# A gated MLP on one core: first casts, weight sums, operand steps and transposes moved to other places in program order

## The chip, the core and the metric

The kernel runs on one core of a Trainium2 chip. The metric is the device time of one execution in microseconds (us); medians and, where small differences matter, means of several executions are given, always beside executions of the kernel before in the same rounds. Every execution also lists the mean clock that was granted to the tensor engine (1.000 is full speed). Engines: PE is the tensor engine, DVE VectorE, ACT ScalarE, POOL GpSimd, SP SyncE, whose queue issues most DMAs.

## The reference

```python
def reference(x, w_gate, w_up, w_down):       # x: 8 x 1024 x 1024, weights 1024 x 4096 and 4096 x 1024
    gate = x @ w_gate
    up = x @ w_up
    gate = 0.5 * gate * (1 + np.tanh(np.sqrt(2 / np.pi) * (gate + 0.044715 * gate ** 3)))
    h = gate * up
    return (h @ w_down).astype(np.float32)
```

## The kernel before

Eight passes of 1024 tokens, each with a gate/up phase (16 pairs of column blocks, 14 products of four matmuls each) and a down phase. It uses fast matrix multiplication (fewer products, more sums): weights and x are added into "operands" first. The first three passes use seven-product sums and, on the side, make the operands for the later passes (w_ops, wd_quads in memory). All of it is scheduled by hand: instructions run on each engine in program order. The parts that the change touches:

The very first pair, before anything is prepared:

```python
def x0_transpose(mh, g, b):                   # PE transposes one block of x, two copies out of PSUM
    ...
    nc.vector.tensor_copy(xq["b11" if mh == 0 else "b12"][:, :, c], ps[:, 0:KH])
    nc.scalar.copy(xq["b21" if mh == 0 else "b22"][:, :, c], ps[:, KH : 2 * KH])

def cast_first(w, kh, cols):                  # float32 weights to float16, on ACT
    nc.scalar.copy(raw(0, 0)[:, w, kh * KH : (kh + 1) * KH, cols], staging0(w, kh)[:, :, cols])
...
for g in range(G):
    x0_transpose(0, g, 4 + g)
    warm(2 if g < G - 1 else 8)               # matmuls on ones, to keep PE's clock up
for kh in range(2):
    for w in range(2):
        cast_first(w, kh, slice(0, 256))
for kh in range(2):
    products(0, kh, slice(0, MH))             # the first 32 products, first half of K first
```

The sums of w_down in the first gate/up phase, placed by product number (14 per pair; `s0 = 28 * n + 59`):

```python
(21, wd_sums, (0,)), (22, wd_sums, (1,)),
(23, wd_sums, (2,)), (24, wd_sums, (3,)), (25, wd_store, (n,)),
```

The operand units of the second and third gate/up phase (a load, then 20 steps, one every six products):

```python
UNITS_ONE = {1: ((0, 60, 6),), 2: ((2, 20, 6),)}    # pass: (unit, product of the load, spacing)
    unit_steps[s0] = load
    unit_steps[s0 + 20 + ds * k] = f
```

The down phase (seven chains v of two chunks nb and four blocks g, one step of eight matmuls each):

```python
steps.setdefault(9 + (17 if i else 0) + 5 * k // 6, []).append(f)    # operand steps
...
if nb == 0 and g == 0 and p + 1 < NPASS:
    ...
    if v == (2 if p < FAST - 1 else 0):       # FAST is 3
        transpose_x(p + 1)                    # four DMA transposes of x on SP's queue
```

## Time and profile before

| | before |
|---|---|
| time, first three runs | 2269.1 us median, 2267.74 to 2269.33 |
| span of the profiled execution | 2265.6 us |
| PE busy | 2249.9 us |
| listed PE waits | 11.6 us, all before 740 us |
| the largest of them | 2.08 us at 389.8, second gate/up phase |

PE is busy nearly all the time, so the profile is read for PE's few waits and for the chain behind each. A wait list gives total, times and longest; the timeline shows in brackets how long an engine stood idle before an instruction and what ended it. The lines are in the prediction below.

### The profile page before, as it was taken

To read this page: it belongs to the slowest core of one execution; us is meant where nothing else is said; L and a number is where in the kernel's file an instruction comes from. 1 tells how busy PE (TensorE), PEld (TensorE's weight loads), DVE (VectorE), ACT (ScalarE), POOL (GpSimd) and SP (SyncE) were. 2 spreads that over 40 slices of the span, in tenths; PEclk is the share of its full clock that TensorE was granted. 3 is DMA by queue.
4 is the path that set the end of the run, shared out by engine and by line. 5 is a ranking of instruction groups with operands and counts; after the bars stand their busy time and mean duration, and the time that the engine had idled before them with its cause. 6 is when DMAs were issued, how large, how long until landed. Compare 5 with 4: busy or idle time off the path is not lost.

```text
span 2265.6 us, 42805 instructions
## 1 busy us (share of the span) xinstructions
PE 2249.9 (99%) x16639; PEld 1625.8 (72%) x16639; DVE 1560.5 (69%) x2188; ACT 956.5 (42%) x1868; POOL 687.4 (30%) x825
## 2 busy tenths in 40 slices
PE   9999999999999999999999999999999999999999
PEld 4444444444444445888888888888888888888888
DVE  5576457874488855777776668666776667866674
ACT  4443135551265522666125551255403553055520
POOL 1343013330133310454105450245402543034520
PEclk9999999999999999999999999999999999999999
DMA  9998969999999999999998989989999889998876
GB/s 232 177 209 205 250 209 223 247 264 284 254 242 238 263 313 342 332 343 373 306 334 279 316 310 303 334 272 322 296 328 321 280 314 312 324 314 277 283 290 228
DMA packets 308092, 642.45 MB, mean 284 GB/s; under 512 B 79088, under 2 KB 185328, under 8 KB 287344
## 3 DMA queue, kind: packets, MB, share of 16 engines
q1 hardware_dynamic: 253104, 566.57, 73.4%
q0 software_dynamic: 54784, 73.14, 19.2%
q8 instruction: 130, 2.13, 0.4%
q14 instruction: 74, 0.61, 0.1%
HBM read 574.36 MB, written 138.41 MB: 315 GB/s over the span
## 4 chain that ended last, share of the span: by engine, by line
PE 91%; DVE 5%; DMA 2%; SPq 1%; issue 1%; ACT 0%; POOL 0%; DVEq 0%; ACTq 0%
PE ps L847 40%; PE ps L1097 20%; PE ps L625 19%; PE ps L989 11%; DVE ring L350 2%; DVE tmp L644 1%; DMA x_sums<-in_w_down_dram 1%; SPq L255 1%; DVE h_s L278 1%; DMA wd_quads<-x_sums 1%; PE ps L1196 1%; DVE h_a L662 1%; DVE x_sums L278 0%; DMA h_a<-in_x_dram 0%; DMA ring<-wd_ops 0%
## 5 line engine op out<-in xcount | busy, mean ns | idle before, releaser
L847 PEld LDWEIGHTS <-ring 128*128 128x128 f16 x8320 | 814.1, 98 | 94.4
L824 POOL TENSOR_TENSOR h_a<-tmp 128x256 f16<-128x256 f32 x640 | 468.5, 751 | 840.1 <-ACT tmp L812 832.8
L847 PE MATMUL ps<-x_sums,ring 128*128 128x256 f16 x5760 | 655.8, 273 | 0.0
L809 DVE TENSOR_TENSOR tmp<-tmp,ps 128x512 f32<-128x512 f32 x640 | 414.4, 683 | 147.4 <-PE ps L847 101.6
L625 PEld LDWEIGHTS <-ring 128*128 128x128 f16 x2632 | 257.4, 98 | 319.4 <-issue 10.9
L794 ACT COPY tmp<-ps 128x512 f32<-128x512 f32 x520 | 303.9, 584 | 237.3 <-PE ps L847 159.5
L625 PE MATMUL ps<-x_sums,ring 128*128 128x512 f16 x1504 | 342.7, 379 | 5.9 <-DVE tmp L644 2.9
L812 ACT ACTIVATE tmp<-tmp 128x256 f32<-128x256 f32 x640 | 263.8, 418 | 173.3 <-DVE tmp L807 79.6
L847 PE MATMUL ps<-x_b,ring 128*128 128x256 f16 x2560 | 305.6, 273 | 0.0
L651 POOL TENSOR_TENSOR h_a<-tmp 128x512 f16<-128x512 f32 x94 | 153.4, 1632 | 375.1 <-ACT tmp L649 254.4
L807 DVE TENSOR_TENSOR tmp<-ps,tmp 128x512 f32<-128x512 f32 x240 | 165.4, 689 | 145.7 <-ACT tmp L794 100.0
L625 PE MATMUL ps<-x_b,ring 128*128 128x512 f16 x1128 | 259.1, 379 | 0.0
L1097 PEld LDWEIGHTS <-h_a 128*128 128x128 f16 x2240 | 219.2, 98 | 25.4
L989 PE MATMUL ps<-ring,h_a 128*128 128x512 f16 x1024 | 222.3, 379 | 0.4 <-DMA ring<-wd_ops 0.4
L1097 PE MATMUL ps<-ring,h_a 128*128 128x256 f16 x1920 | 216.1, 273 | 0.0
L644 DVE TENSOR_TENSOR tmp<-ps,tmp 128x512 f32<-128x512 f32 x188 | 127.4, 684 | 121.4 <-ACT tmp L636 118.5
L989 PEld LDWEIGHTS <-h_a 128*128 128x128 f16 x1152 | 112.7, 98 | 136.6 <-DMA ring<-wd_ops 0.9
L1154 ACT ACTIVATE tmp<-ps 128x512 f32<-128x512 f32 x60 | 35.3, 597 | 362.6 <-PE ps L1097 274.6
L1166 DVE SCALAR_TENSOR_TENSOR tmp<-ps,tmp 128x512 f32<-128x512 f32 x120 | 81.1, 690 | 97.5 <-PE ps L1097 66.7
L636 ACT COPY tmp<-ps 128x512 f32<-128x512 f32 x188 | 109.8, 585 | 86.4 <-PE ps L625 83.3
L350 DVE TENSOR_TENSOR ring<-ring 128x1024 f16<-128x1024 f16 x188 | 133.0, 721 | 9.3 <-DMA ring<-in_w_up_dram 5.1
L1097 PE MATMUL ps<-ring,x_sums 128*128 128x256 f16 x1120 | 126.4, 273 | 0.0
(100 smaller groups left out, 1536.6 us busy)
## 6 DMA issues: line engine op xcount, KB each, us to landing
ring<-w_ops SPq DMA_DIRECT2D x480, 512.0 KB, 5.0
ring<-wd_quads SPq DMA_DIRECT2D x110, 1024.0 KB, 7.0
ring<-wd_ops SPq DMA_DIRECT2D x35, 1024.0 KB, 7.4
out_dram<-tmp SPq DMA_DIRECT2D x128, 256.0 KB, 6.6
w_ops<-h_s SPq DMA_DIRECT2D x128, 256.0 KB, 7.0
ring<-in_w_gate_dram POOLq DMA_DIRECT2D x23, 1024.0 KB, 10.9
ring<-in_w_up_dram POOLq DMA_DIRECT2D x23, 1024.0 KB, 18.4
wd_quads<-x_sums SPq DMA_DIRECT2D x131, 128.0 KB, 5.7
```

What stands on the lines that cost most here:

```text
L350: nc.vector.tensor_tensor(o, a, b, op)
L625: nc.tensor.matmul(ps(b, w), lhs[:, k], rhs[:, k, :], start=(first and k == 0), stop=(k == KH - 1), skip_group_check=True,)
L644: nc.vector.tensor_tensor(o, ps("b", w), o, ADD)
L651: nc.gpsimd.tensor_tensor(hq[TO[n]][:, i, :], tmp[:, t[n, 1]], tmp[:, t[n, 0]], MUL)
L794: nc.scalar.copy(tmp[:, t[o[1]]], ps_all[:, bank[o[2]]])
L807: nc.vector.tensor_tensor(d, b, a, SUB)
L809: nc.vector.tensor_tensor(d, a, b, ADD if o[4] == "add" else SUB)
L812: nc.scalar.activation(d, d, GELU, scale=GSC)
L824: nc.gpsimd.tensor_tensor(h, tmp[:, t[o[1]], MQ : 2 * MQ], g, MUL)
L847: nc.tensor.matmul(ps_all[:, bank[c], w * MQ : (w + 1) * MQ], lhs[:, w, k], rhs[:, k], start=(first and w == 0 and k == 0), stop=(k == KH ...
L989: nc.tensor.matmul(ps_all[:, bank[b, g]], lhs[:, j, g * P : (g + 1) * P], dc[:, n, :], start=(first and j == 0), stop=(j == NP - 1), skip_ ...
L1097: nc.tensor.matmul(ps_all[:, bank[c], m * MQ : (m + 1) * MQ], lhs[:, j, m * P : (m + 1) * P], rhs[:, j, :], start=(first and j == 0 and m ...
```

## The change

Its intent: take away the waits of PE that are left in the first three passes. The diff, its comments and blank lines cut:

```diff
-        nc.scalar.copy(xq["b21" if mh == 0 else "b22"][:, :, c], ps[:, KH : 2 * KH])
+        if mh:
+            nc.scalar.copy(xq["b22"][:, :, c], ps[:, KH : 2 * KH])
+        else:
+            return lambda: nc.scalar.copy(xq["b21"][:, :, c], ps[:, KH : 2 * KH])
...
-    UNITS_ONE = {1: ((0, 60, 6),), 2: ((2, 20, 6),)}
+    UNITS_ONE = {1: ((0, 40, 6),), 2: ((2, 10, 6),)}
...
-                    unit_steps[s0 + 20 + ds * k] = f
+                    unit_steps[s0 + 36 + ds * k] = f
...
-                        (21, wd_sums, (0,)), (22, wd_sums, (1,)),
-                        (23, wd_sums, (2,)), (24, wd_sums, (3,)), (25, wd_store, (n,)),
+                        (18, wd_sums, (0,)), (19, wd_sums, (1,)),
+                        (20, wd_sums, (2,)), (21, wd_sums, (3,)), (23, wd_store, (n,)),
...
-                    steps.setdefault(9 + (17 if i else 0) + 5 * k // 6, []).append(f)
+                    s0 = 26 if i else 9 if p else 4
+                    steps.setdefault(s0 + (5 * k // 6 if p else k), []).append(f)
...
-                        if v == (2 if p < FAST - 1 else 0):
+                        if v == (3 - p if p < FAST - 1 else 0):
...
+        late = []
         for g in range(G):
-            x0_transpose(0, g, 4 + g)
-            warm(2 if g < G - 1 else 8)
-        for kh in range(2):
-            for w in range(2):
-                cast_first(w, kh, slice(0, 256))
+            late.append(x0_transpose(0, g, 4 + g))
+            warm(2 if g < G - 1 else 3)
+        for w in range(2):
+            cast_first(w, 0, slice(0, 256))
+        for f in late:
+            f()
+        for w in range(2):
+            cast_first(w, 1, slice(0, 256), nc.vector.tensor_copy)
```

I call the parts A (the start), B (the w_down sums), C (the first down phase) and D (the operand units), as the prediction does.

More of the change, by code (lines that the diff above doesn't have):

```diff
@@ L325, in load_first, with cast_first @@
         )
-    def cast_first(w, kh, cols):
-        nc.scalar.copy(
-            raw(0, 0)[:, w, kh * KH : (kh + 1) * KH, cols], staging0(w, kh)[:, :, cols]
-        )
+    def cast_first(w, kh, cols, copy=nc.scalar.copy):
+        copy(raw(0, 0)[:, w, kh * KH : (kh + 1) * KH, cols], staging0(w, kh)[:, :, cols])
     def load_raw(p, q):
```

## The prediction

> **What bounds the kernel now.** I read the page's busy shares first, then the tensor engine's waits, then the chain of waits around each of them, then the timelines of the engines named there.
>
> ```profile
> span 2265.6 us, 42805 instructions
> PE 2249.9 (99%) x16639; PEld 1625.8 (72%) x16639; DVE 1560.5 (69%) x2188; ACT 956.5 (42%) x1868; POOL 687.4 (30%) x825
> ```
>
> The tensor engine (PE) works for 2249.9 of 2265.6 us. A change that leaves its matmuls alone can only win from the remaining 15.7 us. 2% of 2269.1 us is 45 us, so "faster by over 2%" is out of reach before any detail is read. What remains is which of PE's few waits go. The list of waits, PE alone (waiting line, what released it: total us, times, longest):
>
> ```profile
> PE ps L625 <- DVE tmp L644: 2.9, 5, 2.1
> PE ps L625 <- DVE ring L350: 1.7, 4, 0.4
> PE ps L1217 <- DVE h_s L1220: 1.6, 1, 1.6
> PE ps L989 <- ACT tmp L914: 1.2, 1, 1.2
> PE ps L1196 <- DVE x_b L305: 1.1, 2, 0.6
> PE ps L625 <- ACT ps L641: 1.1, 2, 0.5
> PE ps L1196 <- ACT ring L328: 1.0, 1, 1.0
> PE ps L303 <- DVE h_a L297: 0.6, 2, 0.4
> PE ps L989 <- DMA ring<-wd_ops: 0.4, 1, 0.4
> ```
>
> They sum to 11.6 us, all before 740 us; the change edits only that part. Four places matter.
>
> **The start.** Chain of waits, first 30 us (start, us, what):
>
> ```profile
> 9.64 0.34 DVE x_b L305
> 10.01 2.05 ACT x_b L306 x4
> 12.06 0.94 ACT ring L328
> 13.05 7.08 PE ps L1196 x32
> ```
>
> ScalarE (ACT) first does four copies of transposed x out of PSUM, and only then casts the first weights, although they need nothing from the copies. The PE's 32 first products start at 13.05 and run at 7.08/32 = 0.221 us each.
>
> **The w_down sums on VectorE (DVE) in the first gate/up phase.** Four times PE waits 0.42 to 0.43 us for a weight sum (L350); the chain before the first shows unrelated sums (h_s, L411 to L415) in between:
>
> ```profile
> 90.79 0.60 DVE h_s L413
> 91.39 0.60 DVE ring L350
> 91.99 0.60 DVE tmp L644
> 92.59 0.60 DVE h_s L415
> 93.19 0.61 DVE ring L350
> ```
>
> **The first down phase.** SyncE's queue, the DVE and the PE timelines (start, us, engine, line; in brackets the idle time before and its releaser):
>
> ```profile
> 249.74 18.59 SPq L255 DMA_TRANSPOSE x_b<-x_half  x4
> ```
> ```profile
> 271.90 0.43 DVE L278 TENSOR_TENSOR x_sums<-x_sums 128x512 f16<-128x512 f16 x1 [19.92 <-DMA wd_quads<-x_sums]
> ```
> ```profile
> 273.89 3.61 PE L989 MATMUL ps<-ring,h_s 128*128 128x512 f16 x16 [1.20 <-ACT tmp L914]
> ```
>
> Four DMA transposes keep the queue for 18.6 us. Operand stores (wd_quads) queue behind them, their buffers stay taken, DVE and ACT stand still, and ACT's next copy out of PSUM (L914) comes 1.20 us too late. A weight load late in the same queue costs 0.41 us at 284.8.
>
> **The second gate/up phase**, chain before 389.8:
>
> ```profile
> 365.29 20.49 DMA x_sums<-in_w_down_dram
> ...
> 385.80 0.43 DVE x_sums L278
> ```
>
> An operand step needs w_down data issued by GpSimd only at 365.3, behind two large loads. DVE blocks on it; everything behind it is late, and PE waits 2.08 us (the "longest" of the first wait line).
>
> **What the Trainium skill says.** (1) "TensorE: Matmul & The Clock Gate", the table at the top: the other engines' queues are strict FIFO, only PE pulls weight loads ahead. The trace agrees: casts whose data had landed sat behind copies, a PSUM copy behind an operand copy. So program order decides here. (2) Same page, Part 1, the HAM clock gate: the PE's clock is halved until about 3.4 us of work, and again after an idle window as long. Here the nine warm-up matmuls take 4.02 us (0.447 each), later ones 0.221. (3) "VectorE: DVE Perf Modes", Mode 2×_2P: copies and scalings of fp32 from SBUF run two elements a cycle. The trace has no such copy on DVE, but the fp32 scaling of 128x1024 (L297) takes 0.69 us, against 1.06 for ACT's cast of the same size. (4) "DMA: Bandwidth & Descriptors", SWDGE vs HWDGE vs iDMA: a transposing DMA must be issued from SP or ACT. So the transposes can be moved in the queue, not to GpSimd; the trace shows them on SP only.
>
> **The change, part by part.**
>
> *A, start.* Five warm-up matmuls leave, the two casts of the first half of K go ahead of ACT's copies, the two of the second half go to DVE. Landing = issue + time to landing: gate 2.60 + 7.8 = 10.4, up 3.08 + 8.8 = 11.9, then second half 3.66 + 9.8 = 13.5 and 4.29 + 10.6 = 14.9.
> - ACT casts gate 10.4 to 11.5, up 11.9 to 13.0, copies x 13.0 to 15.05 (2.05 as before).
> - DVE ends its x copies at 10.97 as before; it casts the second half 13.5 to 14.2 and 14.9 to 15.6, before its next work (x rows landing at 16.2).
> - PE: eight products from 11.5 to 13.3 (8 × 0.221), eight for up to 15.05, eight on the copied x to 16.85 (x is ready at 15.05, just in time), eight to 18.6. Before: 13.05 + 7.08 = 20.13. Gain 1.5.
> - Afterwards: the next x rows are scaled by 18.2, and the next weight columns are landed and cast by 24.7 and about 28.4, while the second pair, moved from 30.16 to about 28.7, needs the latter only two products of 0.87 later. I take 1.4 as surviving. The fewer warm-ups leave a gap from 10.9 to 11.5, far under 3.4 us.
>
> *B, w_down sums* three products earlier, ahead of the pair's own adds; the pair's weight sums then have the end of the pair to themselves. DVE sat idle 5.97 us there. Data: the last chunk of the first group is issued at 71.8 and lands 11.7 later, 83.5, before 85.4, when DVE's next add is ready. Later groups land 12 to 14.5 us after issue; moved with the shorter backlog I get 110.4 against an add at 109.7, a slip below 1 us with about 2 us of slack (four sums of 0.60 cost PE only 0.43). Gain 4 × 0.43 = 1.7.
>
> *C, first down phase.* Operand steps begin at step 4 rather than 9 and come one per step (eight matmuls, 1.735 us) so they end at step 23; transposes start at step 24, about 257 us (phase start 213.7). Both waits go if the queue is free in time: even at 18.6 us the transposes end at 275.6; the load behind them lands 7.4 later, 283.0, and is needed at 213.7 + 40 × 1.735 = 283.1. In the second down phase the same four took 12.57 us, and here a GpSimd load issued at 248.8 will mostly be over, so I expect about 13. Gain 1.2 + 0.4 = 1.6.
>
> *D, operand units in the second and third gate/up phases.* Load at product 40 (was 60), steps from 76 (was 80): 36 products, 31 us, for data that took 20.5, and it now goes ahead of the two large loads. Gain 2.1. But steps also land on other products. The small waits before (0.53, 0.24, 0.20 in this phase, 0.20, 0.52, 0.20 in the next) match steps on product 11 of an even pair (0.52), product 11 of an odd pair (0.20) or 9 of an odd pair (0.24). The new positions have two, one and two of these in the second phase: 1.7 instead of 1.0. In the third, steps from 46 instead of 40 are the same places one step later: unchanged. Loss 0.7.
>
> Sum: 1.4 + 1.7 + 1.6 + 2.1 − 0.7 = 6.1 us. 2269.1 − 6.1 = **2263.0 us**, 0.3% faster.
>
> **Rivals.**
> - *The waits move instead of going.* For: DVE was 10.00 of 10 us busy at 220 to 230 us, exactly where C adds operand steps, and B's later groups have data near their deadline. Against: the sums that PE needs next end by 235 while PE uses them from 241.5 and 248.4. If B fails in three groups of four and C leaves one wait: about 2265.5.
> - *The start is bound by the landing of weights.* For: the second half lands at 13.5 and 14.9, and the old casts began just as it did. If a later PE wait (rows of x, the second pair) swallows the gain, A gives 0.3: 2264.1.
> - *The PE clock drops because fewer warm-ups run.* One 3.4 us window at half clock costs 1.7 us: about 2264.7. Against: the tensor engine is idle only about 0.6 us there, and the old gap of 1.0 us left the clock at full.
> - *Everything goes,* the small waits too, because the blocks behind them are shorter: 0.7 + 1.9 more, about 2260.4.
>
> **Range and chances.** The executions before spread from 2267.74 to 2269.33, so ±0.8 is noise of the base. With the rivals: 2260.0 to 2266.0 eight times in ten. No rival reaches 45 us in either direction: faster 0.01, same 0.98, slower 0.01.
>
> **What would show it.** Right: first products at about 11.5 and the end of the 32 near 18.6; no PE wait on L350's line in the first phase; transposes starting after 255 us and no wait on the PSUM copies or the late load in the first down phase; no 2 us wait in the second gate/up phase but still small ones; PE waits near 5 to 6 us in all. Wrong: a gap inside the first 32 products, matmuls of 0.4 us after 11 us, transposes still holding up a load until after 283, or DVE waiting for h_s data at 106 to 112 us long enough that PE waits again.

## The result, and the profile after

2262.24 us median (2261.5 to 2262.95, six runs) against 2269.1 us (2267.74 to 2270.05, six runs). Ratios here are the mean time of one kernel's fast runs over that of the other's of the same rounds, so not quite the ratio of the medians: 0.997, with a 95% interval of 0.9957 to 0.9983. That is 6.75 us between the means, 2269.02 and 2262.27.

The head of the page of the changed kernel. Its span is 4.5 us shorter, PE's busy time 2.5, of which 5 × 0.214 are the removed warm-ups:

```profile
span 2261.1 us, 42805 instructions
PE 2247.4 (99%) x16634; PEld 1624.9 (72%) x16634; DVE 1565.3 (69%) x2190; ACT 954.6 (42%) x1866; POOL 686.0 (30%) x825
```

PE's waits in the changed kernel. Its line numbers are 1 to 3 higher: L645, L642, L991, L351 are L644, L641, L989, L350 of before.

```profile
PE ps L626 <- DVE tmp L645: 2.2, 7, 0.4
PE ps L626 <- ACT ps L642: 1.9, 4, 0.5
PE ps L1219 <- DVE h_s L1222: 1.6, 1, 1.6
PE ps L303 <- DVE h_a L297: 1.2, 2, 0.9
PE ps L1198 <- DVE x_b L305: 1.1, 2, 0.6
PE ps L991 <- DMA ring<-wd_ops: 0.8, 1, 0.8
PE ps L1198 <- ACT ring L331: 0.6, 1, 0.6
```

They sum to 9.4 us. The 2 us wait is gone, and so are the four on L351. But seven short waits on L645 and four on L642 stand where there were five and two, and the wait for the late load has doubled.

**A.** ACT's timeline, then PE's:

```profile
10.33 1.04 ACT L331 CAST ring<-x_sums 128x1024 f16<-128x1024 f32 x1 [8.10 <-DMA x_sums<-in_w_gate_dram]
11.84 1.04 ACT L331 CAST ring<-x_sums 128x1024 f16<-128x1024 f32 x1 [0.46 <-DMA x_sums<-in_w_up_dram]
12.79 2.04 ACT L309 COPY x_b<-ps 128x512 f16<-128x512 f16 x4
```
```profile
11.43 7.08 PE L1198 MATMUL ps<-x_b,ring 128*128 128x512 f16 x32 [0.58 <-ACT ring L331]
```

The casts now begin as their data land, and the 32 products run from 11.43 without a gap. In this trace the second pair starts at 28.54 instead of 30.16.

**B.** The whole timeline near the first group of sums:

```profile
85.77 0.68 DVE L414 TENSOR_TENSOR h_s<-h_s 128x1024 f16<-128x1024 f16 x1
...
86.33 1.27 POOL L652 TENSOR_TENSOR h_a<-tmp 128x512 f16<-128x512 f32 x1 [6.93 <-ACT tmp L650]
86.37 1.77 DVE L416 TENSOR_TENSOR h_s<-h_s 128x1024 f16<-128x1024 f16 x1
...
92.34 4.48 PE L626 MATMUL ps<-x_sums,ring 128*128 128x512 f16 x20 [0.40 <-DVE tmp L645]
```

The fourth sum takes 1.77 us instead of 0.68. It starts 0.04 us after a GpSimd product and ends 0.54 after it (86.33 + 1.27 = 87.60; 86.37 + 1.77 = 88.14). Then DVE's work is late again, and PE waits 0.40 us, for another DVE instruction than before. This happens in all four groups.

**C.** SP's queue, and PE at the end of the late load:

```profile
263.87 9.82 SPq L255 DMA_TRANSPOSE x_b<-x_half  x4
273.79 0.53 SPq L535 DMA_DIRECT2D ring<-wd_ops  x1
```
```profile
282.35 20.89 PE L991 MATMUL ps<-ring,h_a 128*128 128x512 f16 x96 [0.82 <-DMA ring<-wd_ops]
```

The wait on the PSUM copy is gone. But the transposes start at 263.87, not at 257, because operand stores ahead of them wait for DVE, which waits for stores (7.54 us at 253.1, 5.37 at 261.8). The load behind them is issued at 273.79 and lands 8.5 us later, 0.82 too late.

**D.** PE in the second gate/up phase; the 2.08 us at 389.8 are gone, small waits are left:

```profile
373.53 4.48 PE L626 MATMUL ps<-x_sums,ring 128*128 128x512 f16 x20 [0.34 <-ACT ps L642]
398.41 4.48 PE L626 MATMUL ps<-x_sums,ring 128*128 128x512 f16 x20 [0.52 <-ACT ps L642]
435.22 4.48 PE L626 MATMUL ps<-x_sums,ring 128*128 128x512 f16 x20 [0.20 <-DVE tmp L645]
472.29 4.48 PE L626 MATMUL ps<-x_sums,ring 128*128 128x512 f16 x20 [0.52 <-ACT ps L642]
```

How far the changed kernel is ahead at the same instruction of both traces, read from PE's timelines:

| point | before | after | ahead | gained in this part |
|---|---|---|---|---|
| second pair begins | 30.16 | 28.54 | 1.62 | A 1.62 |
| after the fourth group of sums | 168.06 | 166.54 | 1.52 | B −0.10 |
| second gate/up phase begins | 312.46 | 309.98 | 2.48 | C 0.96 |
| third gate/up phase begins | 607.12 | 602.66 | 4.46 | D 1.98 |
| last small wait of that phase | 732.44 | 727.55 | 4.89 | D 0.43 |

Over the rest, which the change does not touch, 0.44 are lost again, so the spans differ by 4.45. D's 2.41 are more than the listed waits give (2.08 − 0.61). The rest are stalls inside runs of matmuls: before, four runs of 24 matmuls took 5.54 to 5.70 us instead of 5.34; after, one.

The two traces are 4.5 us apart, the timed means 6.75. That is the first question for the experiments.

### The profile page after: what moved, and what is told of

Same layout as the page of the kernel before. It is cut to its first block, busy times and chain, and to the rows that moved or that the text cites. A ratio compares the mean times of both kernels' runs of the same rounds, so it can differ in the third digit from the quotient of the medians.

```text
span 2261.1 us, 42805 instructions
## 1 busy us (share of the span) xinstructions
PE 2247.4 (99%) x16634; PEld 1624.9 (72%) x16634; DVE 1565.3 (69%) x2190; ACT 954.6 (42%) x1866; POOL 686.0 (30%) x825
## 4 chain that ended last, share of the span: by engine, by line
PE 84%; DVE 3%; DMA 2%; SPq 0%; issue 0%; ACT 0%; DVEq 0%
PE ps L848 40%; PE ps L1099 20%; PE ps L626 14%; PE ps L991 10%; DMA wd_quads<-x_sums 1%; DVE ring L351 1%; DVE h_s L278 1%; DVE tmp L645 1%; DMA w_ops<-h_s 1%; SPq L255 0%; DMA ring<-wd_ops 0%; DVE x_sums L278 0%; DVE h_a L663 0%; ACT ps L642 0%; DVE h_a L923 0%
## 5 line engine op out<-in xcount | busy, mean ns | idle before, releaser
L991 PE MATMUL ps<-ring,h_a 128*128 128x512 f16 x1024 | 222.3, 379 | 0.8 <-DMA ring<-wd_ops 0.8
L991 PEld LDWEIGHTS <-h_a 128*128 128x128 f16 x1152 | 112.7, 98 | 137.0 <-DMA ring<-wd_ops 1.3
L645 DVE TENSOR_TENSOR tmp<-ps,tmp 128x512 f32<-128x512 f32 x188 | 127.2, 683 | 107.0 <-ACT tmp L637 104.1
L351 DVE TENSOR_TENSOR ring<-ring 128x1024 f16<-128x1024 f16 x188 | 133.1, 722 | 8.7 <-DMA ring<-in_w_up_dram 4.5
```

Of the source, the lines that this page charges most:

```text
L351: nc.vector.tensor_tensor(o, a, b, op)
L645: nc.vector.tensor_tensor(o, ps("b", w), o, ADD)
L991: nc.tensor.matmul(ps_all[:, bank[b, g]], lhs[:, j, g * P : (g + 1) * P], dc[:, n, :], start=(first and j == 0), stop=(j == NP - 1), skip_ ...
```

## The experiments

Each was timed in five rounds. Since sets ran at different times and on different chips, I compare differences to the kernel before in the same rounds; the changed kernel's own is −6.75 us. Mean differences and the clocks of the five runs:

| run | mean, us | to before | clock below 1.000 |
|---|---|---|---|
| A alone | 2266.11 | −2.90 | 0 of 5 |
| B alone | 2268.22 | −0.79 | 1 of 5 |
| C alone | 2270.59 | +1.58 | 5 of 5 |
| D alone | 2265.65 | −3.36 | 1 of 5 |
| changed, sums at one place | 2261.16 | −8.50 | 0 of 5 |
| changed, transposes behind the load | 2262.01 | −7.65 | 0 of 5 |
| C alone, transposes behind the load | 2266.22 | −3.44 | 1 of 5 |
| changed, three moves | 2259.93 | −9.73 | 0 of 5 |
| changed, second casts on ACT | 2263.59 | −4.45 | 0 of 5 |
| changed, eight warm-ups | 2264.61 | −3.42 | 2 of 5 |
| changed, two moves | 2259.56 | −8.48 | 0 of 5 |
| changed without C | 2263.79 | −4.90 | 0 of 5 |

An interval of a ratio is some ±0.13%, ±3 us, because the kernel before itself spreads over 2266.5 to 2273.4. So traces decide, and times only where they differ by several us. The four parts alone add up to −5.5 us by this table, against −6.75 together: no conflict at this noise.

**Each part alone.** The kernel before with one part of the diff, nothing else.

A alone:

> Only the start of the first pair is changed (casts of the first half of K ahead of ACT's copies, the second half on DVE, five warm-ups fewer). The prediction gave this 1.4 us, the traces of before and after show the second pair starting 1.6 us earlier (30.16 and 28.54). Theory: the parts are independent and this one is worth 1.4 to 1.8 us, about 2267.4. Rival (a later wait swallows it): within 0.3 us of before.

2265.73 us median, ratio 0.9987 (0.9974 to 1.0001). The 32 products start at 11.89 here, because the x rows landed later in this execution; from the first transposes after that wait to the first product it is 3.2 us (8.70 to 11.89), as in the changed kernel (8.25 to 11.43) and unlike before (4.6 us, 8.43 to 13.05). The second pair still starts about 1.4 us sooner after those transposes than before, and no later PE wait in this trace has grown to swallow it: the rival is out by the trace (the interval of the time alone would still allow it). The wait on the PSUM copy in the first down phase shrank to 0.15 us by itself in this trace, so that wait is not fixed either.

B alone:

> Only the w_down sums of the first phase are moved three products earlier. Prediction: 1.7 us less, because the four PE waits of 0.42 us on the weight sums go. The trace of after shows four waits of 0.40 us on another DVE instruction in their place. Theory now: worth 0.1 us, four waits of 0.40 us remain and the fourth sum takes 1.77 us beside a GpSimd product. Rival (the predicted one, the waits of after come from another part of the change): 1.7 us less and no such wait.

2267.7 us, ratio 0.9996 (0.9983 to 1.0008). Four waits of 0.40 us on L644, none on L350: B alone swaps one wait for another, and no other part is to blame.

C alone:

> Only the first down phase is changed (operand steps from step 4, one per step, the transposes behind them). Prediction: 1.6 us less. The trace of after shows the 1.20 us wait gone and the wait for the late load grown from 0.41 to 0.82, so 0.8 us less. Rival: the timed runs of before and after lie 6.9 us apart and the two traces 4.5; if waits in this phase differ between executions, because transposes share the DMA engines with other traffic, this part alone is worth 2 to 4 us in the timed runs.

2270.35 us, ratio 1.0006 (0.9994 to 1.0019): not the gain of 0.8 that I expected, though the interval alone doesn't show a loss either. PE's timeline, from two stretches:

```profile
286.24 22.58 PE L990 MATMUL ps<-ring,h_a 128*128 128x512 f16 x96 [2.77 <-DMA ring<-wd_ops]
```
```profile
392.84 6.16 PE L625 MATMUL ps<-x_sums,ring 128*128 128x512 f16 x20 [1.99 <-DVE tmp L644]
```

The wait for the late load is 2.77 us, and the 96 matmuls behind it take 22.58 us where 20.89 is normal; the 20 behind the wait of 1.99 us take 6.16 instead of 4.48. Both are 1.7 us too long. The stretches just behind them; columns are the stretch, its length, busy time (and instructions) of PE, its weight loads, DVE, ACT and POOL, then the granted clock, the DMA share and GB/s:

```profile
286.20:289.60 3.40, 3.36 (x11) 1.36 (x12) 1.03 (x2) 0.00 (x0) 0.00 (x0) 0.67 1.03 400
...
393.00:396.40 3.40, 3.40 (x10) 1.24 (x9) 3.40 (x5) 1.12 (x3) 1.85 (x2) 0.53 1.00 148
```

The first stretch starts too early and mixes full and half clock. Read in steps of 0.4 us, the granted clock is 0.50 from about 287.4, 1.2 us after PE resumed, to about 290.8, and from about 393.2 to 396.6: twice 3.4 us, and 3.4 × 0.5 = 1.7. (The listed clock has a blind spot: for the first 4 us of the kernel before it says 1.00, though the warm-up matmuls take 0.447 us each instead of 0.221.) This is what the timed runs of before hide: in the four sets of nine, 25 runs list 1.000 (mean 2268.1), nine 0.999 (2270.0) and two 0.998 (2273.0). The profiled execution of before was a clean one. The 0.74 us by which the mean of all 36 (2268.85) exceeds that of the 25 are the clock's part of the average; the changed kernel and six of its variants (all but the one with eight warm-ups) have 36 runs of 36 at 1.000. The rest of the gap between traces and times, about 1.5 us, is spread: one clean trace of before was 0.8 below its clean mean, the trace of after 0.6 above its mean.

D alone:

> Only the positions of the operand units in the second and third gate/up phases are changed. Prediction: 2.1 us less for the wait on w_down data, 0.7 us more for small waits, 1.4 in sum; the trace of after gives 2.1 and 0.6. Theory: 1.4 to 1.5 us less. Rival: the wait on w_down data is longer than 2.1 us in the timed runs (its load lands 20 us after issue among other traffic), then 2.5 to 4 us less.

2265.19 us, ratio 0.9984 (0.9972 to 0.9997), the one part whose interval lies clear of 1. Its trace has no 2 us wait. The mean time is 3.4 us lower, as the rival had it, but the rival's reason does not hold: the wait is 1.7 to 2.1 us in every trace that has it. I put the rest down to the clock and to stalls too short to be listed; that is argued, not shown, as the interval (0.7 to 6.3 us) holds 1.4 as well. One of five runs still lists 0.999, which its trace (longest wait there 1.6 us, at the very start) doesn't explain.

**The sums.** The Trainium skill's page "SBUF — State Buffer", section "SBUF: two separate sides", says that DVE and GpSimd share one port pair under an exclusive lock, taken by a DVE operation with two SBUF inputs against a GpSimd operation that reads SBUF, and that the loser blocks fully. That fits roughly: blocked until the product's recorded end (1.23 us) and then running its usual 0.68, the sum would take 1.91 us; it took 1.77, 0.14 less. A control stands in the trace of before: at 88.29 a DVE instruction with one input in PSUM (L662) ran inside such a product (87.75 to 89.02) in its usual 0.69 us. The test puts all four sums before that product:

```diff
-                        (18, wd_sums, (0,)), (19, wd_sums, (1,)),
-                        (20, wd_sums, (2,)), (21, wd_sums, (3,)), (23, wd_store, (n,)),
+                        (18, wd_sums, (0,)), (18, wd_sums, (1,)),
+                        (18, wd_sums, (2,)), (18, wd_sums, (3,)), (23, wd_store, (n,)),
```

> The changed kernel with all four w_down sums at the first of their four places, so that the fourth does not start beside GpSimd's product. Theory (the fourth sum, 1.77 us instead of 0.68, is what made the predicted 1.7 us of the sums fail): all sums take 0.68 to 0.70, the four waits of 0.40 us go, 1.6 us less than the changed kernel, about 2260.7. Rival (VectorE simply has too much to do at the end of those pairs, or the data lands too late): the waits stay near 0.4 and the time at 2262.2.

2261.27 us, ratio 0.9963 (0.9949 to 0.9977). The sums of its first two groups (min, median, max in ns):

```profile
L410 DVE TENSOR_TENSOR h_s<-h_s x2: 691/691/691, 81.1 to 105.6; 128x1024 f16<-128x1024 f16 x2
L412 DVE TENSOR_TENSOR h_s<-h_s x2: 693/693/693, 82.4 to 106.9; 128x1024 f16<-128x1024 f16 x2
L414 DVE TENSOR_TENSOR h_s<-h_s x2: 683/683/683, 83.0 to 107.5; 128x1024 f16<-128x1024 f16 x2
L416 DVE TENSOR_TENSOR h_s<-h_s x2: 682/682/683, 83.6 to 108.1; 128x1024 f16<-128x1024 f16 x2
```

None is long, and no PE wait of that phase is left: the mechanism that B was meant to have works once the collision is gone. The data lands in time, so the rival falls. The test moves the second and third sum as well, so it does not isolate the collision; but in the changed kernel the fourth sum lost 1.09 us and the wait was 0.40, so by the trace's sum the collision alone is enough. The time is 1.1 us lower by the means (1.75 by the differences to before). Of the 1.6 us expected, 0.4 are given back: PE reaches the late load of the first down phase earlier, and that wait is 1.22 us here instead of 0.82.

**The queue.** The transposes one chunk later for the first down phase, behind the load in program order:

```diff
-                    if nb == 0 and g == 0 and p + 1 < NPASS:
+                    if nb == (0 if p else 1) and g == 0 and p + 1 < NPASS:
```

On the changed kernel:

> The changed kernel with the transposes issued one chunk later, behind the load that the tensor engine waits for. Theory: the wait for the load (0.82 us) goes, 0.8 us less than the changed kernel, about 2261.4, and the scaling of x is not late. Rival (the load is slow because of traffic and not because of its place in the queue): a wait of some tenths stays; or the transposes land too late and a new wait appears where x is scaled or in the second gate/up phase.

2262.1 us, ratio 0.9967 (0.9954 to 0.9979). The wait for the load is gone from the trace (load issued at 264.1, transposes 13.0 us from 264.6), and nothing new appears; x is scaled at 283.1, in the changed kernel at 282.8. The time is 0.3 to 0.9 us lower, depending on whether times or differences to before are compared: shown as a wait, unproven as a time.

On C alone:

> The kernel before with the part of the first down phase alone, and the transposes behind the load. The same part without that move measured 2270.35 against 2269.11, with a wait of 2.77 us, and its trace shows the tensor engine at half clock for 3.4 us after that wait and again after one of 1.99 us; every one of its runs lists a clock below 1. Theory (a wait of 2 us or more can drop the clock and costs up to 1.7 us more): without that wait 1.6 us less than before, about 2267.5, with clocks like those of before (some runs at 0.999, from the wait in the second gate/up phase that this kernel keeps). Rival (the clock drops for another reason): the clock is below 1 in every run again.

2266.16 us, ratio 0.9985 (0.9973 to 0.9998), against 2270.35 for C alone. Neither down-phase wait is in its trace, and one clock in five is below 1 instead of five. That is lower than the 2267.5 expected, within the noise. So C costs only through the late load and what the clock adds to it.

All three moves (the third: operand steps of the second gate/up phase at load + 40 instead of + 36):

> The changed kernel with both moves, and the operand steps of the second gate/up phase four products later, on the places that they had before. Theory: 1.6 + 0.8 + about 0.4 (small waits of 1.6 us in that phase become 1.2) = 2.8 us less than the changed kernel, about 2259.4, all clocks at 1.000. Rival (the moves give each other's gain back): above 2260.5.

2259.72 us, ratio 0.9958 (0.9945 to 0.997), lower than both kernels, near the 2259.4 expected. But its trace has a new wait of 1.61 us at 457.4, behind a late load of gate/up weights. So I took the third move back:

> The changed kernel with the two moves that worked alone (all w_down sums at their first place, transposes behind the load) and the operand units as the change has them. The three moves together gave 2259.7, with a new wait of 1.61 us in the second gate/up phase in its trace. Theory: that wait came from the moved operand steps or from a late load of weights there; without the move 1.0 + 0.8 us less than the changed kernel, about 2260.3, and no wait above 0.6 us there. Rival: the same wait appears here too, so it is not the move's.

2259.65 us (2258.47 to 2260.37), ratio 0.9964 (0.9951 to 0.9976): the same time without the third move, and the longest wait of that phase is 0.61. This is the version I would keep. Whether the third move made the new wait is open. C alone shows one of 1.52 us at the same place with the steps where they were before, but the kernel before, A alone and B alone, with the same places too, show 0.2 us there: chance in the landing of that load is likelier than the places.

**The start in halves.** The changed kernel with the second half's casts left on ACT (`cast_first(w, 1, slice(0, 256))`):

> The changed kernel with the casts of the second half of K left on ACT, behind its copies of x. Tells the two halves of the start apart. From the trace of the changed kernel: ACT is free at 14.8, two casts would end at 15.8 and 16.9; the tensor engine, ready for them at 15.0 and then 8 products later, would wait about 0.8 us and then 0.0 to 0.1, so the 32 products end about 0.9 us later and the time is 0.9 us above the changed kernel's. Rival (only the order of the first casts matters, later waits absorb the rest): within 0.2 us of the changed kernel.

2263.47 us, ratio 0.9981 (0.9969 to 0.9994). PE's timeline:

```profile
11.19 3.63 PE L1198 MATMUL ps<-x_b,ring 128*128 128x512 f16 x16 [0.60 <-ACT ring L331]
15.55 3.63 PE L1198 MATMUL ps<-x_b,ring 128*128 128x512 f16 x16 [0.73 <-ACT ring L331]
```

The 32 products now have a gap of 0.73 us in the middle and end at 19.18, 7.99 us after they began instead of 7.08: 0.9 as expected. The time is 1.3 us higher by the means (2.3 by the differences); the wait for the late load, 1.04 us instead of 0.82, is part of that. Both halves of A count: the move to DVE for 0.9, the reordering together with the fewer warm-ups for the rest, some 0.6 to 0.7.

Eight warm-ups again (`warm(2 if g < G - 1 else 8)`):

> The changed kernel with eight warm-up matmuls after the last transposes again, as before. Theory: they only stand in the way, by 5 x 0.214 less the idle 0.58 us, so the first products start 0.5 us later and the time is 0.5 us up; the clock needs them not. Rival (the predicted fear, fewer warm-ups let the clock drop): the time falls.

2264.0 us, ratio 0.9986 (0.9973 to 1.0). The rival is out: the time rises. From the last transposes to the first products 2.19 us pass (9.49 to 11.68) instead of 1.85 (9.58 to 11.43): the warm-ups cost 0.34, a little less than the 0.5 expected. The rest of the 2.3 us is no matter of warm-ups: in this trace the wait for the late load is 2.41 us, and two of five clocks are below 1.

**C taken back** from the changed kernel:

> The changed kernel with the part of the first down phase taken back (operand steps from step 9, transposes at step 16), the other three parts kept. Alone this part cost 1.2 us; in the trace of the changed kernel it gains 0.8. Theory: in company it is worth little, 0 to 0.8 us, because the wait for the late load takes the place of the wait on the PSUM copies: 2262.2 to 2263.1. Rival (it costs in company too): 2261 or below, with clocks at 1.000.

2263.79 us, ratio 0.9977 (0.9964 to 0.9991). In company C is worth 1.5 us by the means (1.9 by the differences to before), alone its mean is 1.6 higher (within the interval); the expected 0 to 0.8 is missed. In the trace without C the two waits of before are 0.59 and 0.40, hardly more than the 0.82 that C leaves, so the traces don't show where the 1.5 us come from. What differs between C in company and C alone is the wait for the late load: 0.82 to 1.22 us in the changed kernel and two variants, where the four transposes keep the queue for 9.8 to 10.8 us, but 2.77 in C alone and 2.41 with eight warm-ups, where they keep it for 11.4 and 11.6. Why they take longer there stays open.

## Why the prediction was right, and where not

The time, 2262.24, lies in the range and 0.8 us from the point; the class is right. The parts are less good than the sum: PE's listed waits fell by 2.2 us to 9.4, not to the 5 to 6 that the prediction gave as a sign of being right.

- *What bounds the kernel:* right. PE stays at 99%, no gain could be large.
- *A, 1.4 us:* right in mechanism and size. Casts at the landing times foreseen (10.33 and 11.84 for 10.4 and 11.9), DVE's two casts at 0.69 us each for 0.7, products at 11.43 for 11.5, their end 0.1 us from the forecast, 1.62 us kept at the second pair (0.12 of it because rows of x landed earlier: from the last transposes to the first products it is 3.35 us before, 1.85 after).
- *B, 1.7 us:* this step failed, B gained nothing in the trace. "The pair's weight sums then have the end of the pair to themselves" and "about 2 us of slack" left out that the fourth sum would meet GpSimd's product. It lost 1.09 us to it, and the waits came back at 0.40 us each under another name. This is the prediction's own first rival, waits that move instead of going, in four groups of four. The deadline of the data, which I had worried about, held.
- *C, 1.6 us:* the wait on the PSUM copy went as said; "Both waits go" failed for the late load, whose wait grew from 0.41 to 0.82. Mis-sized was the queue: transposes "at step 24, about 257 us" (step 24 is 255.3 by the prediction's own figures) came at 263.87, and the load landed after 8.5 us and not 7.4. The kernel before had shown the delay: its transposes stand at step 16, 241.5 by the same figures, and started at 249.74, behind operand stores. That the four transposes took 9.82 us and not the expected 13 was luck; otherwise the deadline would have been missed by some 3 us more. Gained in the trace 0.96, in company by the times 1.5.
- *D, 2.1 − 0.7:* the wait went. The small waits rose by 0.61 where 0.7 was foreseen, but not at the places counted: the two of 0.24 did not come, and one of 0.34 at 373.5 did, which D alone and four other traces with the same places don't have. There the second gate/up phase has 0.52, 0.20 and 0.52, 0.27 more than before, so the agreement is luck. The gain was larger, 2.41 in the trace, for stalls too short to be listed had been left out.
- *The clock:* the rival feared it at the start, where fewer warm-ups did no harm. It does drop, but behind waits of about 2 us, and the kernel before pays for it in 11 of 36 runs. That gain of about 0.7 us on average was in no term of the sum. It made up for part of what B and C failed to bring.

So the sum was right partly by luck, because errors cancelled: B 1.8 and C 0.6 too much in the trace, D 1.0 and the clock 0.7 too little.

## What to carry to other kernels

When an engine is 99% busy, the last waits are moved more easily than removed: after each move, ask what else runs at the new place, on which shared port and behind which queue, and look whether the wait came back under another name. A wait of about 2 us of the tensor engine can cost nearly as much again in clock, and not in every execution, so one trace against timed means can miss it: read the clock that each run lists.

## What the Trainium skill lacked or had wrong

- "TensorE: Matmul & The Clock Gate", Part 1, has the clock fall after an idle window of about 3.4 us. Here it fell to half behind waits of 2.77 and 1.99 us, for 1.7 us of loss each; waits of 1.6 to 2.4 us in other traces passed without it. Which of them trigger it stays open.
- No page gives the time for which DMA transposes keep the issuing queue beside other traffic ("DMA: Bandwidth & Descriptors" has a bandwidth, and cycle counts without the data transfer). The same four kept it for 9.8 to 18.9 us in these runs' first down phase, and a 1 MB load right behind them was 0.8 to 2.8 us late.
